# A two-layer encoder with grouped experts: the overflow branch placed at the layer's end

## The chip, the core and the metric

The kernel runs on one core of a Trainium2 chip. The core has five engines that run their own instruction queues side by side and wait for each other by semaphores: TensorE (PE, matrix products), VectorE (DVE), ScalarE (ACT), GpSimd (POOL) and SyncE (SP), which here only issues transfers. Transfers run on 16 DMA engines. The metric is the device time of one execution in microseconds; the median of several runs counts.

## The reference

The program is two layers over 512 tokens of width 1024, all in float32. A layer has a mixer and a grouped mixture of experts, each with a residual sum and a layer norm:

```
for i in range(DEPTH):                      # DEPTH = 2
    z = x @ w_in                            # token mixer and query of a memory attention
    o = concat([tok, xa]) @ w_out[i]
    x = layer_norm(ALPHA * x + o)
    f = grouped_moe(x, router_w, router_b, w_gate[i], w_up[i], w_down[i])
    x = layer_norm(ALPHA * x + f)

def grouped_moe(x, ...):                    # 16 experts in 4 groups, two experts per token
    ...                                     # sigmoid scores, best group, top 2 inside it
    for e in range(N_EXPERTS):
        h = jax.nn.silu(xt @ w_gate[e]) * (xt @ w_up[e])
        out = out + combine[:, e:e + 1] * (h @ w_down[e])
```

`w_gate` and `w_up` are 1024 x 512 per expert and layer, `w_down` 512 x 1024: 6 MB of weights per expert, 16 experts, two layers.

## The kernel before

**Experts.** Each expert takes up to 128 tokens. `route` and `tables` make for every expert a list of its tokens' rows (`idxs`) and their gates. `experts` (L650) then runs the 16 experts in a loop: `gather(e)` fetches the tokens' rows from DRAM through GpSimd, `xtrans(e)` transposes them on TensorE and splits them, `gate_up(e)` makes gate and up and multiplies them into `h`, `htrans(e)` transposes `h` into `ht`, `down(e)` makes the down product, and `scatter(e)` adds its rows to a copy of the residual stream in DRAM, `rd[i]`. `down(e - 1)` comes behind `gate_up(e)`; in the last expert it comes in the middle of `gate_up(15)`. The last expert's own product isn't scattered: `selt`, a matrix of ones and zeros that says which token sits in which of its slots, is made from `posp`, and `total` (L781) adds on TensorE the rows read back from `rd[i]`, and `selt` times the product.

**Precision.** Every product is made of three (`mm3`, L202 to L204): both operands are split into a high part that TensorE's fast float32 mode takes and a low rest. ScalarE makes the high part (a copy, L168 for weights, L207 for activations), VectorE the rest (a subtraction, L169 and L208).

**Weights.** A `Stream` W loads weights in tiles of 1 MB (`raw`) through SyncE, in the order of use, into pages of on-chip memory; there are 24 pages for everything. `W.keep` is the number of pages that loads must leave free, `W.flight` the number of loads under way, `W.stop` how many tiles of the next layer wait until its end. `W.rings(8)` sets pages aside for split tiles (`high`, `low`). Whenever a tile's use ends, `W.done` calls `pump`, which splits the next raw tile and issues the next load.

**More than 128 tokens.** `overflow` counts on TensorE (L603) how many tokens each expert has and makes `nover`, the number of full sets of 128 over the first, on VectorE (L605 to L610). `more` (L893 on) loads `nover` into a register of every engine's queue, compares it with zero, and only if it is larger runs a loop that handles the rest, one expert at a time, with gathers, products, weight loads of its own and a scatter-add to `rd[i]`. In the profiled execution no instruction of that loop's body ran: each queue jumps over it. Before, `more` is called between `fill` and the expert loop, with the page `hy` for its scratch. `fill` is in layer 0 the keys and values of the next layer's memory attention (`keys_values`, L315), in layer 1 nothing.

**The order of the work.** A planner of the compiler orders each engine's instructions by a simulated timeline, earlier program text first where it can. `tc.issue_after(ins)` keeps what a block issues behind `ins` on that instruction's engine. Inside `tc.manual_schedule(...)` the listed engines keep the program's order. The expert loop is in such a block for TensorE, ScalarE and VectorE; before, `order.close()` ends it ahead of the last expert, whose gate, up and `down(14)` the planner orders freely. The layer's end (from `htrans(last)` on) is in a second such block, with eight small warm-up products (`keep_warm(8)`) held behind the last product of gate and up. A conditional block is one unit for the planner: nothing from outside is put among its instructions.

Of the kernel before, what the change touches and what calls it, by code (L numbers as in the profile page):

```python
# [18 lines left out]
FT = mybir.dt.float32  # L19
FR = mybir.dt.float32r  # L20
# [3 lines left out]
OP = mybir.AluOpType  # L24
# [3 lines left out]
P = 128  # L28
D = 1024
KB = D // P  # L30
S = 512
NC = S // P
# [5 lines left out]
FE = 512  # L38
# [9 lines left out]
def trunk(ctx, tc, x, mem, w_in_a, sgu_ln_g, sgu_ln_b, sgu_w, sgu_b, w_in_b, conv_w, w_kv, w_out,  # L48
          ln1_g, ln1_b, router_w, router_b, w_gate, w_up, w_down, ln2_g, ln2_b, out):
    nc = tc.nc  # L50
    vec, act, pool_e, pe, sp = nc.vector, nc.scalar, nc.gpsimd, nc.tensor, nc.sync
# [12 lines left out]
    def page(name, shape, dtype=FT, of=None):  # L64
        of = free_pages if of is None else of
        assert of, f"no page for {name}; held: {sorted(v[1] for v in held.values())}"
        i = of.pop(0)
        uid[0] += 1
        t = pages.tile(shape, dtype, name=f"{name}_{uid[0]}", tag=f"pg{i}", bufs=1)
        held[id(t)] = (i, name, t)  # L70
        return t

    def drop(*ts):
        for t in ts:
            i, name, _ = held.pop(id(t))
            W.home(name).append(i)
# [4 lines left out]
    def bank(shape, name="bank"):  # L81
        return psum.tile(shape, FT, name=name, tag="B", bufs=3)
# [115 lines left out]
    W = Stream()  # L198

    def mm3(o, a, b, start, stop):  # L200

        pe.matmul(o, a[0], b[0], start=start, stop=False)  # L202
        pe.matmul(o, a[0], b[1], start=False, stop=False)  # L203
        return pe.matmul(o, a[1], b[0], start=False, stop=stop)  # L204
# [7 lines left out]
    ident = consts.tile([P, P], FT, name="ident")  # L212
# [40 lines left out]
    slot1 = consts.tile([P, P], FT, name="slot1")  # L253
# [41 lines left out]
    def keep_warm(n):  # L295

        t = bank([P, 4, P], "warm")
        for _ in range(n):
            pe.matmul(t, ones_b, ones_b[:, None, :].to_broadcast([P, 4, P]), start=True, stop=True)
# [12 lines left out]
    memh = page("memh", [P, KB, NMEM], FR)  # L312
    meml = page("meml", [P, KB, NMEM], FR)
# [5 lines left out]
    def keys_values(after=None):  # L319
        kt = page("kt", [P, 2, H, NMEM], FR)  # L320
        vt = page("vt", [P, 2, 2, MW], FR)
        a = [acc("ka") for _ in range(H)]
        for j in range(4):
            g = W.next()
            for kk in range(2):
                k = 2 * j + kk
                for h in range(H):
                    cs = slice(h * P, (h + 1) * P)
                    mm3(a[h][:, :NMEM], (g[:, 0, kk, cs], g[:, 1, kk, cs]), (memh[:, k, :], meml[:, k, :]),
                        k == 0, k == KB - 1)  # L330
            W.done(g)
        for h in range(H):
            split_to(kt[:, 0, h, :], kt[:, 1, h, :], a[h][:, :NMEM])
        a = [acc("va") for _ in range(2)]
        for j in range(4):
            g = W.next()
            for kk in range(2):
                k = 2 * j + kk
                for m in range(2):
                    ms = slice(m * P, (m + 1) * P)  # L340
                    with ExitStack() if after is None or j < 3 else tc.issue_after(after):
                        mm3(a[m], (memh[:, k, ms], meml[:, k, ms]), (g[:, 0, kk, :], g[:, 1, kk, :]),
                            k == 0, k == KB - 1)
            W.done(g)
        for m in range(2):
            split_to(vt[:, 0, m, :], vt[:, 1, m, :], a[m])
        return kt, vt

    def x_transposed():
        xh = [page("xh", [P, 4, S], FR) for _ in range(2)]  # L350
# [155 lines left out]
    posp = consts.tile([P, NC, E], FT, name="posp")  # L506
# [144 lines left out]
    def experts(i, lnp, fill, after, stop, fine=False):  # L651

        last = E - 1
        xg = page("xg", [P, 2, D])
        pool_e.memset(xg, 0.0)
        hy = page("h", [P, 4, FE])
# [15 lines left out]
        def xtrans(e):  # L672
            for q in range(2):
                t = bank([P, 4, P], "xt")
                for k in range(4):
                    k0 = 4 * P * q + 2 * P * (k // 2) + k % 2
                    pe.transpose(t[:, k, :], xg[:, e % 2, k0:k0 + 2 * P - 1:2], ident)  # L677
                split_to(xt[:, 0, 4 * q:4 * q + 4, :], xt[:, 1, 4 * q:4 * q + 4, :], t)
# [26 lines left out]
        def down(e, evict):  # L705
            for n in range(2):
                o = acc("ya")
                for j in range(2):
# [5 lines left out]
                        evict(n, o)  # L714
                    W.done(g)

        def scaled(e):
            return lambda n, o: act.activation(ys[e % 2][:, n * 512:(n + 1) * 512], o, AF.Copy, scale=tabs[e][1])  # L718

# [2 lines left out]
        if i:  # L722
            with tc.issue_after(last_entry[-1]):
                keep_warm(8)
        fill()
        more(i, hy)
        W.keep, W.flight = 0, 4
        W.ahead, W.whole, W.on_pool = 6, True, lambda n: False
        W.rings(8)
        xtrans(0)  # L730
        gather(2)
        W.pump()
        order = ExitStack()
        order.enter_context(tc.manual_schedule(engines={ET.PE, ET.Activation, ET.DVE}))
        for e in range(E):
            if e == last:
                order.close()
            up = gate_up(e, (lambda: (down(last - 1, scaled(last - 1)), scatter(last - 1))) if e == last else None)
            if e + 1 < E:
                xtrans(e + 1)  # L740
            if e + 3 < E:
                gather(e + 3)
            if e == 5:
                W.parts += 2
            if 0 < e < last:
                down(e - 1, scaled(e - 1))
                scatter(e - 1)
            if e == last - 3:
                W.keep = 4
                W.stop = stop - 2 if stop else 0  # L750
            if e == last:
                W.rings(0)
                drop(xt, xg)
                selp = page("selt", [P, 2, NC, P], FT)
                for c in range(NC):
                    vec.tensor_scalar(selp[:, 0, c, :], slot1, posp[:, c, last:last + 1], None, op0=OP.is_equal)
                t = bank([P, NC, P], "selt")
                for c in range(NC):
                    pe.transpose(t[:, c, :], selp[:, 0, c, :], ident)
                selt = page("selr", [P, NC, P], FR)  # L760
                vec.tensor_copy(selt, t)
                drop(selp)
                xs[:] = [page("x", [P, 2, D]) for _ in range(2)]
                xrow[:] = [xs[c // 2][:, c % 2, :] for c in range(NC)]
                with tc.issue_after(added[last - 1].ins):
                    lnp = ln_params(*lnp, pool_e)
                for c in range(NC):
                    W.behind = sp.dma_start(xrow[c], rd[i][c * P:(c + 1) * P, :]).ins
            if e < last:
                htrans(e)  # L770
# [63 lines left out]
            moments(c)  # L834

        with tc.manual_schedule(engines={ET.PE, ET.Activation, ET.DVE, ET.Pool}):
            with tc.issue_after(up.ins):
                keep_warm(8)
            htrans(last)
            keep_warm(4)  # L840
            down(last, parts)
            act.activation(lnp[:, 0], lnp[:, 0], AF.Copy, scale=ALPHA)
            if fine:
                for c in range(3):
                    total(c)
                half_moments(0)
                part(1, 0)
                finish(0, "pool")
                after(0)
                part(1, 1)  # L850
                total(3)
                moments(1)
                centred(1)
                finish(1, "both")
                after(1)
                half_moments(2)
                centred(2)
                finish(2, "split")
                after(2)
                half_moments(3)  # L860
                centred(3)
                finish(3, "vec")
                after(3)
            else:
                total(0)
                total(1)
                half_moments(0)
                centred(0)
                finish(0, "dve")
                total(2)  # L870
                half_moments(1)
                centred(1)
                finish(1, "dve")
                after(0)
                total(3)
                W.after = after(1).ins
                half_moments(2)
                if "both" != "pool":
                    centred(2)
                finish(2, "both")  # L880
                half_moments(3)
                if "split" != "pool":
                    centred(3)
                finish(3, "split")
# [95 lines left out]
    W.after = last_mem.ins  # L980
    W.pump()
    W.after = None
    kt, vt = keys_values()
    xh, xl = x_transposed()
    for c in range(NC):
        transposed(xrow[c], KB, lambda q: xh[q], lambda q: xl[q], c * P)
# [5 lines left out]
    t = bank([P, 12], "cwt")  # L992
    pe.transpose(t, cwr, ident[:12, :12])
    act.activation(cw.rearrange("p t b -> p (t b)"), t, AF.Copy)
    t = bank([P, H, P], "sgt")
# [78 lines left out]
    def fill0():  # L1074
        W.on_pool = lambda n: False
        kv1.append(keys_values(last_entry[-1]))
        drop(memh, meml)
    xhl = []

    def next_x(c):  # L1080
# [2 lines left out]
        xh, xl = xhl[0]  # L1083
        return transposed(xrow[c], KB, lambda q: xh[q], lambda q: xl[q], c * P)
    experts(0, (ln2_g[0], ln2_b[0]), fill0, next_x, stop)
    kt, vt = kv1[0]
    xh, xl = xhl[0]


# [69 lines left out]
```

## Time and profile before

| | |
|---|---|
| three timed runs | 1032.32, 1035.75, 1035.86 us; median 1035.75 |
| profiled execution | 1031.97 us, of which the span from first to last instruction is 1030.1 us |
| TensorE busy | 983.7 us (95%), weight loads of TensorE 810.6 us (79%) |
| VectorE, ScalarE, GpSimd busy | 774.2 (75%), 627.7 (61%), 200.5 us (19%) |
| mean granted clock of TensorE | 0.973 |
| moved by DMA | 273.30 MB, mean 265 GB/s |
| expert loop, layer 0 and layer 1 | about 213 to 500 us and 706 to 998 us of the span |

Times in rows are microseconds from the span's start. A timeline row has start, duration, engine, line, operation, what it writes and reads, how many instructions were merged, and in brackets the idle time ahead of it with what ended it. PE is TensorE, PEld its weight loads, a q behind an engine's name its queue's own instructions (register loads, branches, semaphores, DMA issues). Durations of matrix products overlap: one of 0.39 us starts 0.23 us after the one before it.

### The profile page before, as it was taken

Reading aid. Unit: us, or ns where it says so; the run is one execution under the profiler, and the core shown is the slowest. Engines: PE = TensorE matmul, PEld = TensorE weight load, DVE = VectorE, ACT = ScalarE, POOL = GpSimd, SP = SyncE. Lnnn points to the kernel's source line nnn. Section 1 sums busy time; section 2 is a strip of 40 time slices with the busy share of each in tenths; the row PEclk is TensorE's granted clock in tenths of the full one; section 3 lists DMA queues with packets and bytes.
Section 4 is the critical chain, followed back from the end, with each engine's and each line's share of the span. In section 5 each row is a group of like instructions: output and inputs, shape, how many; then the busy total and the mean of one; then the engine's idle time right before and its main releaser. Section 6 shows DMA issues by size and latency. Waiting matters only on the chain. (4 is left out here: it accounts for less than half of the span.)

```text
span 1030.1 us, 12721 instructions
## 1 busy us (share of the span) xinstructions
PE 983.7 (95%) x4815; PEld 810.6 (79%) x4816; DVE 774.2 (75%) x884; ACT 627.7 (61%) x684; POOL 200.5 (19%) x111
## 2 busy tenths in 40 slices
PE   8999999969999999999999999977899999999995
PEld 6788888858888888888679887865688888888873
DVE  4738567867989898898894455675689898988975
ACT  4626532556788787878643414233687887878763
POOL 0000002112332413321110000221133324233023
PEclk9999999989999999999999999987899999999998
DMA  9813266667999999999880425490799999999944
GB/s 321 294 42 123 91 237 247 244 225 265 364 367 333 366 360 360 360 357 362 282 320 1 164 82 207 131 396 25 232 330 362 372 327 383 359 362 355 357 87 160
DMA packets 102219, 273.30 MB, mean 265 GB/s; under 512 B 10442, under 2 KB 10966, under 8 KB 102152
## 3 DMA queue, kind: packets, MB, share of 16 engines
q1 hardware_dynamic: 89480, 242.84, 64.5%
q0 software_dynamic: 11808, 26.97, 9.4%
q10 hardware_dynamic: 864, 2.62, 0.7%
q8 instruction: 39, 0.64, 0.2%
q14 instruction: 28, 0.23, 0.1%
HBM read 262.22 MB, written 26.21 MB: 280 GB/s over the span
## 5 line engine op out<-in xcount | busy, mean ns | idle before, releaser
L169 DVE TENSOR_TENSOR low<-raw,high 128x2048 fp32r<-128x2048 f32 x189 | 427.9, 2288 | 80.9 <-ACT high L168 79.4
L168 ACT ACTIVATE high<-raw 128x2048 fp32r<-128x2048 f32 x189 | 355.1, 1910 | 22.7 <-PE ga L204 10.1
L668 POOL DMA_INDIRECT xg<-x1d,idxs x32 | 83.2, 2601 | 299.6 <-PE xt L677 270.5
L168 ACT ACTIVATE split<-raw 128x1024 fp32r<-128x1024 f32 x66 | 68.9, 1058 | 71.1 <-PE za L204 26.0
L202 PE MATMUL ya<-high,ht 128*128 128x512 f32 x256 | 103.8, 406 | 0.0
L169 DVE TENSOR_TENSOR split<-raw,split 128x1024 fp32r<-128x1024 f32 x61 | 73.6, 1221 | 39.6 <-ACT split L168 38.9
L204 PE MATMUL ga<-high,xgt 128*128 128x512 f32 x248 | 99.1, 399 | 2.9 <-DVE xgt L208 2.9
L204 PE MATMUL ya<-high,ht 128*128 128x512 f32 x256 | 101.3, 396 | 0.1
L203 PE MATMUL ya<-low,ht 128*128 128x512 f32 x256 | 101.1, 395 | 0.0
L202 PE MATMUL ga<-high,xgt 128*128 128x512 f32 x248 | 100.7, 406 | 0.1
L203 PE MATMUL ga<-low,xgt 128*128 128x512 f32 x248 | 98.4, 397 | 0.0
L204 PE MATMUL ua<-high,xgt 128*128 128x512 f32 x248 | 97.1, 392 | 0.0
L202 PE MATMUL ua<-high,xgt 128*128 128x512 f32 x248 | 96.9, 391 | 0.0
L203 PE MATMUL ua<-low,xgt 128*128 128x512 f32 x248 | 96.8, 390 | 0.0
L169 POOL TENSOR_TENSOR split<-raw,split 128x1024 fp32r<-128x1024 f32 x5 | 11.9, 2383 | 267.0 <-DVE sto L475 147.0
L202 PE MATMUL za<-xh,split 128*128 128x512 f32 x160 | 61.6, 391 | 2.0 <-ACT xh L207 2.0
L203 PE MATMUL za<-xl,split 128*128 128x512 f32 x160 | 62.5, 391 | 0.0
L204 PE MATMUL za<-xh,split 128*128 128x512 f32 x160 | 61.5, 389 | 0.0
L204 PEld LDWEIGHTS ga<-high,xgt 128*128 128x128 f32 x248 | 47.4, 191 | 14.1 <-DVE xgt L208 4.0
L204 PEld LDWEIGHTS ya<-high,ht 128*128 128x128 f32 x256 | 48.1, 188 | 12.8 <-DVE ht L208 1.3
L664 POOL DMA_INDIRECT rd<-h,idxs x16 | 40.4, 2523 | 89.3 <-ACT h L718 79.6
L202 PEld LDWEIGHTS ya<-high,ht 128*128 128x128 f32 x256 | 48.4, 189 | 10.5 <-ACT ht L207 0.6
(250 smaller groups left out, 1886.2 us busy)
## 6 DMA issues: line engine op xcount, KB each, us to landing
raw<-in_w_gate_dram SPq DMA_DIRECT2D x64, 1024.0 KB, 9.8
raw<-in_w_up_dram SPq DMA_DIRECT2D x64, 1024.0 KB, 9.6
raw<-in_w_down_dram SPq DMA_DIRECT2D x64, 1024.0 KB, 10.5
raw<-in_w_kv_dram SPq DMA_DIRECT2D x8, 1024.0 KB, 7.4
raw<-in_w_out_dram SPq DMA_DIRECT2D x8, 1024.0 KB, 8.0
raw<-in_w_in_b_dram SPq DMA_DIRECT2D x8, 1024.0 KB, 11.1
raw<-in_w_in_a_dram SPq DMA_DIRECT2D x6, 1024.0 KB, 5.4
x1d<-x POOLq DMA_DIRECT2D x8, 512.0 KB, 6.0
```

The source lines that it names most:

```text
L168: act.activation(high, src, AF.Copy)
L169: (pool_e if self.on_pool(self.count) else vec).tensor_tensor(low, src, high, op=OP.subtract)
L202: pe.matmul(o, a[0], b[0], start=start, stop=False)
L203: pe.matmul(o, a[0], b[1], start=False, stop=False)
L204: return pe.matmul(o, a[1], b[0], start=False, stop=stop)
L664: added[e] = pool_e.indirect_dma_start(out=rd[i], out_offset=bass.IndirectOffsetOnAxis(ap=tabs[e][0], axis=0), in_=ys[e % 2], in_offset=No ...
L668: pool_e.indirect_dma_start(out=xg[:, e % 2], out_offset=None, in_=x1d[i], in_offset=bass.IndirectOffsetOnAxis(ap=tabs[e][0], axis=0), bou ...
```

## The change

The call of `more` moves from ahead of the expert loop to the layer's end, behind the last expert's gate and up and ahead of the loads of the rows from `rd[i]`, and gets a page of its own. With the branch gone from the start, layer 0's first transposes are held behind the last product of `keys_values` by `issue_after`. The block in the program's order now closes behind the last expert's gate, up and `down(14)`. The last expert's slots are compared on VectorE at the start of expert 14 and transposed at the start of expert 15, and one page more is kept free from expert 12 on.

```diff
@@ keys_values @@
-                        mm3(a[m], (memh[:, k, ms], meml[:, k, ms]), (g[:, 0, kk, :], g[:, 1, kk, :]),
-                            k == 0, k == KB - 1)
+                        end = mm3(a[m], (memh[:, k, ms], meml[:, k, ms]), (g[:, 0, kk, :], g[:, 1, kk, :]),
+                                  k == 0, k == KB - 1)
...
-        return kt, vt
+        return kt, vt, end.ins
@@ experts @@
+        def last_slots():
+
+            selp = page("selt", [P, 2, NC, P], FT)
+            for c in range(NC):
+                vec.tensor_scalar(selp[:, 0, c, :], slot1, posp[:, c, last:last + 1], None, op0=OP.is_equal)
+            return selp
+
+        def last_tokens(selp):
+
+            t = bank([P, NC, P], "selt")
+            for c in range(NC):
+                pe.transpose(t[:, c, :], selp[:, 0, c, :], ident)
+            selt = page("selr", [P, NC, P], FR)
+            vec.tensor_copy(selt, t)
+            drop(selp)
+            return selt
...
-        fill()
-        more(i, hy)
+        end = fill()
...
-        xtrans(0)
+        with ExitStack() if i else tc.issue_after(end):
+            xtrans(0)
...
         for e in range(E):
+            if e == last - 1:
+                selp = last_slots()
             if e == last:
-                order.close()
+                selt = last_tokens(selp)
             up = gate_up(e, (lambda: (down(last - 1, scaled(last - 1)), scatter(last - 1))) if e == last else None)
...
             if e == last - 3:
-                W.keep = 4
+                W.keep = 5
...
             if e == last:
                 W.rings(0)
                 drop(xt, xg)
-                selp = page("selt", [P, 2, NC, P], FT)
...
-                drop(selp)
+                order.close()
+                rest = page("more", [P, 4, FE])
+                more(i, rest)
+                drop(rest)
                 xs[:] = [page("x", [P, 2, D]) for _ in range(2)]
...
         with tc.manual_schedule(engines={ET.PE, ET.Activation, ET.DVE, ET.Pool}):
-            with tc.issue_after(up.ins):
-                keep_warm(8)
+            keep_warm(8)
             htrans(last)
```

The callers only hand the third value of `keys_values` through (`fill0` returns it, the others drop it).

## Rows read from the trace of the kernel before

**Rows 1.** Stretch: PE, PEld, DVE, ACT, POOL busy (instructions), clock, DMA share, GB/s
```profile
200.00:216.00 16.00, 7.59 (x39) 6.11 (x38) 9.80 (x18) 8.12 (x8) 2.44 (x3) 0.84 0.59 198
780.00:940.00 160.00, 160.00 (x752) 132.78 (x751) 140.76 (x91) 129.34 (x108) 49.73 (x19) 1.00 1.00 361
```

**Rows 2.** Timeline around layer 0's branch: start, duration, engine, line, operation, idle before
```profile
204.17 1.08 POOL L668 DMA_INDIRECT xg<-x1d,idxs  x1 [22.48 <-DVE gates L635]
...
205.80 4.50 DVE L169 TENSOR_TENSOR low<-raw,high 128x2048 fp32r<-128x2048 f32 x2 [2.38 <-ACT high L168]
...
211.73 0.14 DVE L610 CAST nover<-ovn 1x1 int32<-1x1 f32 x1
212.94 1.28 ACT L207 ACT_TABLE_LOAD   x1 [6.38 <-ACTq L894]
...
213.43 1.95 PE L677 MATMUL xt<-ident,xg 128*128 128x128 f32 x8 [7.40 <-DVEq L894]
...
215.20 0.69 DVE L208 TENSOR_TENSOR xgt<-xt,xgt 128x512 fp32r<-128x512 f32 x1 [3.33 <-ACT xgt L207]
...
216.24 0.63 PE L204 MATMUL ga<-split,xgt 128*128 128x512 f32 x1
...
217.86 0.39 PE L202 MATMUL ga<-split,xgt 128*128 128x512 f32 x1
```

**Rows 3.** First gather, from issue to landing: layer 0, then layer 1
```profile
DMA to landing us min/median/max: 4.2/4.2/4.2
...
DMA to landing us min/median/max: 4.3/4.3/4.3
```

**Rows 4.** Timeline around layer 1's branch, and the stall at its second expert
```profile
701.36 1.08 POOL L668 DMA_INDIRECT xg<-x1d,idxs  x1 [6.09 <-DVE gates L635]
...
706.02 1.95 PE L677 MATMUL xt<-ident,xg 128*128 128x128 f32 x8 [2.12 <-PEq L894]
...
710.22 2.29 DVE L169 TENSOR_TENSOR low<-raw,high 128x2048 fp32r<-128x2048 f32 x1 [0.88 <-PE ga L204]
...
724.21 1.11 PE L702 MATMUL htr<-ident,h 128*128 128x128 f32 x4 [3.51 <-DVE h L693]
```

**Rows 5.** The branch's instructions on TensorE's queue in layer 1
```profile
L893 PEldq TENSOR_LOAD <-nover x1: 312/312/312, 704.6 to 704.6; - x1
...
L894 PEldq COMPARE_BRANCH  x1: 318/318/318, 705.1 to 705.1; - x1
```

**Rows 6.** Waits of SyncE's queue: us in total, times, longest
```profile
SPq L894 <- SPq L894: 7.5, 3, 6.4
```

**Rows 7.** Timeline at layer 1's end, from the last product of "up" to the sums
```profile
998.04 1.90 PE L299 MATMUL warm<-ones_b 128*128 128x512 bf16 x8
998.31 0.69 DVE L693 TENSOR_TENSOR h<-h,ua 128x512 f32<-128x512 f32 x1 [0.69 <-PE ua L204]
998.91 2.28 DVE L169 TENSOR_TENSOR low<-raw,high 128x2048 fp32r<-128x2048 f32 x1
...
999.78 0.60 PE L702 MATMUL htr<-ident,h 128*128 128x128 f32 x4
...
1000.99 2.13 SPq L768 DMA_DIRECT2D x<-rd  x3
...
1007.10 1.02 PE L785 MATMUL ra<-x,ident 128*128 128x512 f32 x2
```

**Rows 8.** Timeline of VectorE at layer 0's end
```profile
501.31 2.28 DVE L169 TENSOR_TENSOR low<-raw,high 128x2048 fp32r<-128x2048 f32 x1
...
503.51 0.68 DVE L208 TENSOR_TENSOR ht<-htr,ht 128x512 fp32r<-128x512 f32 x1
...
505.24 2.29 DVE L169 TENSOR_TENSOR low<-raw,high 128x2048 fp32r<-128x2048 f32 x1 [1.05 <-ACT high L168]
```

**Rows 9.** Waits of SyncE's queue in layer 0's loop: 222 to 420, then 440 to 460
```profile
SPq L147 <- DVE low L169: 119.9, 47, 7.9
...
SPq L147 <- DMA raw<-in_w_up_dram: 11.1, 3, 4.7
```

More of the change, by code (lines that the diff above doesn't have):

```diff
@@ L753, in experts @@
                 drop(xt, xg)
-                selp = page("selt", [P, 2, NC, P], FT)
[L755 to L761, printed above, removed]
-                drop(selp)
+                order.close()
+                rest = page("more", [P, 4, FE])
+                more(i, rest)
+                drop(rest)
                 xs[:] = [page("x", [P, 2, D]) for _ in range(2)]
@@ L982, in trunk @@
     W.after = None
-    kt, vt = keys_values()
+    kt, vt, _ = keys_values()
     xh, xl = x_transposed()
@@ L1077, in fill0 @@
         drop(memh, meml)
+        return kv1[0][2]
     xhl = []
@@ L1085, in trunk @@
     experts(0, (ln2_g[0], ln2_b[0]), fill0, next_x, stop)
-    kt, vt = kv1[0]
+    kt, vt, _ = kv1[0]
     xh, xl = xhl[0]
```

## The prediction, made before the changed kernel was run

> **What bounds the kernel now.** I read the page's first two parts, then the stretches of each stage, then the instructions around the branch and at both layers' ends, and last the waits of the load queue. In the page TensorE is busy 95% of 1030.1 us; by stretches it works without a gap through nearly all of both expert loops (160.00 of 160.00 us between 780 and 940, granted clock 1.00, VectorE 140.76) [rows 1]. What this change can win or lose is therefore TensorE's idle time at the loops' two ends, unless it slows the loop itself.
>
> At the start of layer 0's loop the branch holds everything. The memory projection ends near 206.0; TensorE's next work is the first transposes at 213.43, 7.40 us idle, released by VectorE's queue at the branch. The branch needs `nover`, and VectorE makes it last, at 211.87, behind two subtractions of split weights (4.50 us from 205.80) [rows 2]. In that stretch TensorE works 7.59 of 16 us and the clock averages 0.84 [rows 1]. The first gather is issued at 204.17 and lands 4.2 us later, so at 208.4 its rows were there, 5.0 us before anyone was allowed to use them [rows 2, 3].
>
> Layer 1 looks alike and is not. The load of `nover` into TensorE's register starts at 704.6 [rows 5] and the transposes at 706.02, but the gather is issued at 701.36 and lands 4.3 us later, at 705.66 [rows 3, 4]. The branch costs 0.36 us there. The 3.51 us that TensorE waits later, before 724.21, begin with a subtraction at 710.22 that waits for TensorE's first gate tile (for its page), so this chain moves only when TensorE's start moves [rows 4].
>
> **The change, part by part.**
>
> *Layer 0's start.* The load of the register, the compare, the jump and the small steps that make `nover` leave TensorE's path. What is late next? TensorE may transpose at 208.4. Its third matrix product, however, needs the low half of the transposed tokens, a subtraction on VectorE (0.69 us) that started at 215.20; the product followed at 216.24 [rows 2]. VectorE's two weight subtractions wait for pages that the projection frees near 205.8, before the tokens are there, so I expect the planner to leave them and the two value subtractions in front: VectorE is then free at 211.9, where it made `nover`, the low half is done at 211.9 + 0.69 = 212.6, and the third product moves from 216.24 to 212.6: -3.6 us. If the tokens go between the two weight subtractions, VectorE is free for them about 2.3 us earlier (half of 4.50), and the gain is 5.9. On the other side stands the clock: after the 7.4 us of idle the product at 216.24 takes 0.63 us and the one at 217.86 0.39, the lower and the higher level [rows 2]. TensorE would still be idle for some 2.4 us and then again until 212.6, and the clock may fall all the same and stay low for longer than it does now; eight more products at 0.24 us extra take 1.9 from the gain. Bounds -1.7 and -5.9; I take -3.6, nearest to the order that the trace has.
>
> *Layer 1's start.* The gather's landing is the next wait: -0.3 us, between 0 and -0.4. ScalarE's table load behind the branch (1.28 us in layer 0 [rows 2]) goes too, beside other work.
>
> *The loop.* It starts earlier as a whole. Loads in layer 0 wait first for pages that VectorE frees (119.9 us of waits from 222 to 420), later for earlier loads alone (from 440 on) [rows 9]: DMA becomes the tighter stream, and its slack shrinks. Since its first loads in the loop wait for VectorE, they move with TensorE, and the later state is the same one, shifted. I cost the loop at nothing; if that cover fails, the gain at layer 0's start comes back as stalls at its end, up to +3.6. One page more kept back for the last three experts: those loads wait for earlier loads, not pages, so nothing. The slots' comparisons and transposes move from expert 15 to 14: same instructions, and VectorE has 19 us in 160 free [rows 1].
>
> *Layer 1's end.* The branch now stands between the last product of "up" and the last expert's down product. Its price on TensorE's queue: load 0.31, compare and jump 0.32, and from 704.6, where the load starts, to the next instruction at 706.02 it is 1.4 us in all [rows 4, 5]. Before, eight warm-up products began at 998.04, the moment the last product was through, and transposes followed at 999.78 [rows 7]. After, the warm-up is in program order behind the branch: 998.04 + 1.4, and everything behind it, down product, sums, normalization, stores, is 1.4 later; no gap stands before the sums at 1007.10 that could take it up. VectorE also loses the planner's order: the last weight subtraction (2.28 us) comes before the product `h`, not after (998.31 against 998.91 [rows 7]). It starts where VectorE idles for 0.69 us ahead of 998.31 [rows 7], so `h` ends at 997.62 + 2.28 + 0.69 = 1000.6 instead of 999.0, still before 1001.2, when TensorE would take it. Queued behind the branch on SyncE are the loads of the rows; these wait for the last scatter-add anyway and start at 1000.99 [rows 7]. Cost +1.4; at least 0 (if TensorE meets the branch while it waits for something else), at most 2.5.
>
> *Layer 0's end.* The same 1.4 on TensorE, but VectorE has more in front of the branch. Program order there is: weight subtraction, `h`, one more subtraction for the next layer's first weights, branch, low half of `ht`. In the trace the planner put that subtraction behind `ht` (505.24 behind 503.51) [rows 8]. `h` and the weight subtraction of 501.31 only change places; what stands newly in front of `ht` is that other subtraction, 2.29, and the branch, 1.0 (ScalarE's took 1.07, from `nover` to its table load at 212.94 [rows 2]), together 3.3, less 0.3 because the first subtraction doesn't wait for "up" as `h` does: +3.0 us, and the down product's third step waits for it. If the planner sets the branch elsewhere, 0.5; at most 4.
>
> Sum: -3.6 - 0.3 + 3.0 + 1.4 = +0.5 us. The profiled execution took 1031.97 (span 1030.1 and 1.9 around it), so 1032.5 by that account. The three timed runs lie at 1032.32, 1035.75 and 1035.86; with the profiled one, two near 1032 and two near 1035.8. I cannot tell which way the next median falls, take the middle, 1034.0, and predict 1034.5.
>
> **Rivals.**
>
> *A missed jump on the path (slower).* SyncE's queue waited three times for itself at the old branch, 7.5 us in all and 6.4 the longest, while TensorE's needed 1.4 for everything [rows 4, 6]; SyncE had no free page then, and nobody missed it. At the layer's end ScalarE, VectorE and TensorE are all on the path, and one of them pausing as SyncE did costs 6.4 less the 1.0 to 1.4 already counted: +5 to 1039.5 for one, 1044.5 for both layers. For it: that row. Against: SyncE's part of the body, with 24 loads, is the longest to jump over. It decides as soon as a pause on one of these three exceeds about 5 us. The Trainium skill ("Runtime: NRT & Kernel Launch", Instruction fetch mechanics) has a rule that speaks for this rival: a taken branch whose target isn't in the pages of code already fetched stalls until the page has come. SyncE's row agrees with it; by it alone each of the three engines could pay this at each layer's end.
>
> *The start gains more and the ends are hidden (faster).* Token subtractions between the weight ones (-5.9), -0.3, and each branch met while the engine waits for `h` or the rows, +0.4 each: -5.4, 1028.6. For it: greedy planning and idle time before 205.80. Against: the planner's own order in [rows 2].
>
> *The branch isn't where the text puts it.* It is one unit for the planner, which may set later work ahead of it, as the trace shows for weight splits in front of the old branch [rows 2]. Then layer 0's order on VectorE stays mild, the ends cost 0.5 + 0.5, sum -2.9: 1031.1.
>
> **How the numbers follow.** Forecast 0.50, branch elsewhere 0.10, faster rival 0.22, slower rival 0.18. A measurement of this kernel tells about 0.5% (5.2 us) from no change. The faster rival lies on that border: three quarters of it and a little of the others make 0.21 faster; most of the slower one and a tail of the forecast's make 0.20 slower; 0.59 between. For the likeliest alone the start's bounds put the sum between -1.8 and +2.4, and the runs scatter by 1.8 to either side of 1034.0: 1030.4 to 1038.2. Up to the edges of both rivals it is 1028.5 to 1040.
>
> **What will show it.** TensorE's gap before layer 0's first transposes: 2.4 instead of 7.4 us. VectorE's token subtraction there: near 211.9 (right) or before 210 (faster rival). Behind the last "up" product: 1.4 us without work on TensorE in both layers. Layer 0's `ht` subtraction about 3 us further behind "up" than before. A queue's self-wait over 5 us on ScalarE, VectorE or TensorE speaks for the slower rival. The forecast is wrong if TensorE has gaps in the middle of a loop, or if layer 1's start moves by more than half a us.

## The result and the profile after

The changed kernel took 1037.05 us (median of 16 runs, 1034.75 to 1039.24), the kernel before 1032.34 in the same runs (16 runs, 1029.28 to 1035.86): a ratio of 1.0052, 95% interval 1.0038 to 1.0065. It is slower by 0.5%, 4.7 us; 1034.5 had been predicted, half a microsecond over a base of 1034.0, so no difference that can be told. The base was 1.7 us above the 1032.34 that the kernel before took beside it: by luck that brings the absolute figure nearer (2.6 us off) than the difference (4.2 off). The profiled execution has a span of 1035.4 us, 5.3 more than before.

The loops are what they were. Columns as in [rows 1], which the first and third line answer:

```profile
200.00:216.00 16.00, 11.14 (x47) 8.43 (x47) 10.19 (x19) 8.37 (x8) 3.50 (x3) 0.80 0.63 219
500.00:524.00 24.00, 22.47 (x79) 13.71 (x79) 13.76 (x24) 9.24 (x14) 0.00 (x0) 0.86 1.03 377
780.00:940.00 160.00, 160.00 (x753) 132.75 (x752) 140.94 (x91) 128.35 (x108) 49.03 (x18) 1.00 1.01 361
```

TensorE works more at layer 0's start (11.14 us in place of 7.59) and has no gap in the middle of a loop; new is a granted clock of 0.86 where layer 0 ends.

Layer 0's start, which answers to [rows 2] (timeline: start, duration, engine, line, operation, idle before):

```profile
205.69 4.50 DVE L169 TENSOR_TENSOR low<-raw,high 128x2048 fp32r<-128x2048 f32 x2 [2.40 <-ACT high L168]
...
208.18 1.20 PE L677 MATMUL xt<-ident,xg 128*128 128x128 f32 x8 [2.25 <-DMA xg<-x1d,idxs]
...
211.42 1.27 DVE L208 TENSOR_TENSOR xgt<-xt,xgt 128x512 fp32r<-128x512 f32 x2
...
212.14 0.80 PE L204 MATMUL ga<-split,xgt 128*128 128x512 f32 x1 [1.39 <-DVE xgt L208]
```

TensorE's gap is 2.25 us and ends with the gather, and the third product comes at 212.14 in place of 216.24.

Layer 0's end, which answers to [rows 8], with TensorE's rows added:

```profile
493.44 4.50 DVE L169 TENSOR_TENSOR low<-raw,high 128x2048 fp32r<-128x2048 f32 x2 [0.51 <-ACT high L168]
...
495.93 0.39 PE L204 MATMUL ua<-high,xgt 128*128 128x512 f32 x1
497.85 0.68 DVE L693 TENSOR_TENSOR h<-h,ua 128x512 f32<-128x512 f32 x1
498.45 2.28 DVE L169 TENSOR_TENSOR low<-raw,high 128x2048 fp32r<-128x2048 f32 x1
...
500.84 3.60 PE L299 MATMUL warm<-ones_b 128*128 128x512 bf16 x8 [4.53 <-DVEq L907]
...
504.23 1.06 PE L702 MATMUL htr<-ident,h 128*128 128x128 f32 x4
...
505.96 0.69 DVE L208 TENSOR_TENSOR ht<-htr,ht 128x512 fp32r<-128x512 f32 x1 [5.23 <-ACT ht L207]
```

And the branch's instructions there (count, ns, first and last start), TensorE's queue and then VectorE's; they answer to [rows 5]:

```profile
L907 PEldq EVENT_SEMAPHORE  x2: 51/51/51, 496.4 to 496.6; - x2
...
L907 PEldq COMPARE_BRANCH  x1: 228/228/228, 493.6 to 493.6; - x1
```
```profile
L907 DVEq EVENT_SEMAPHORE  x2: 21/21/21, 500.8 to 500.9; - x2
```

TensorE's last "up" product ends at 496.3. Its jump is through at 496.6, because its queue had read and compared `nover` while the products still ran. But the warm-up behind the jump starts at 500.84, when VectorE jumps, and VectorE jumps only after two weight subtractions, `h`, and a third subtraction. After 4.53 us without work the eight warm-up products take 3.60 us, where those of [rows 7] take 1.90: the clock is at its lower level. Then come the transposes, then `ht`.

Layer 1's end, answering to [rows 7]: the same wait, 2.33 us, and the clock is still up behind it (1.90 us for eight products):

```profile
998.14 4.49 DVE L169 TENSOR_TENSOR low<-raw,high 128x2048 fp32r<-128x2048 f32 x2 [0.51 <-ACT high L168]
1002.55 0.68 DVE L693 TENSOR_TENSOR h<-h,ua 128x512 f32<-128x512 f32 x1
...
1003.35 1.90 PE L299 MATMUL warm<-ones_b 128*128 128x512 bf16 x8 [2.33 <-DVEq L907]
...
1005.08 0.60 PE L702 MATMUL htr<-ident,h 128*128 128x128 f32 x4
```

Where the 5.3 us went is read by setting TensorE's instructions of two traces side by side. The table gives, in us against the profile before, what each stage adds: A up to the transposes of `h` in expert 14 of layer 0; B to those of expert 15; C to the first token transposes of layer 1; D to expert 14 of layer 1; E to expert 15; F to the first sum (each number is the difference of two starts, after minus before, less that of the stage ahead). The profiled executions of the four kernels marked * are 1.8 to 2.1 us late from 42 us on, at instructions that are the same in all; their granted clock is 0.83 between 40 and 50 us, where the others but one have 1.00. That is scatter of single executions, and it stands in A. The one, that of the warm-up in other buffers, is 3.2 us late from 64 us on for a reason of its own, told with it, and regains 1.9 at layer 0's start. In the kernels marked w the eight warm-up products left their place behind the last "up" product (both ends; in "only layer 0's branch moved" that of layer 1 alone): the first experiment shows what that does to B, E and F.

| kernel | A | B | C | D | E | F | median us | ratio to before (95%) |
|---|---|---|---|---|---|---|---|---|
| changed | -4.3 | +6.4 | +2.3 | -1.1 | +2.0 | -0.1 | 1037.1 | 1.0052 (1.0038 to 1.0065) |
| no branch * w | -2.5 | +2.5 | +2.2 | -0.9 | +2.0 | +1.3 | 1034.6 | 1.0028 (1.0011 to 1.0044) |
| warm-up in other buffers | -2.9 | +3.0 | +1.4 | -0.9 | +0.4 | 0.0 | 1035.1 | 1.0032 (1.0019 to 1.0045) |
| subtractions behind | -6.4 | +1.5 | +1.0 | -1.5 | +1.2 | -0.1 | 1029.7 | 0.9981 (0.9969 to 0.9994) |
| only layer 0's branch moved w | -4.6 | +6.3 | +2.4 | -1.1 | +2.0 | +1.3 | 1038.2 | 1.0057 (1.0037 to 1.0077) |
| order alone * w | -0.3 | +2.4 | +4.6 | +0.4 | +2.0 | +1.2 | 1041.4 | 1.0092 (1.0067 to 1.0116) |
| move alone * | -2.3 | +7.9 | +1.8 | +0.3 | +2.2 | 0.0 | 1039.7 | 1.0070 (1.0047 to 1.0092) |
| behind, branch at the start * w | +2.9 | +1.0 | +1.1 | -0.7 | +0.6 | +0.2 | 1034.5 | 1.0027 (1.0011 to 1.0044) |
| behind, warm-up ahead | -4.9 | +0.6 | +1.1 | -1.1 | +0.1 | 0.0 | 1028.1 | 0.9963 (0.9945 to 0.9981) |
| the same, layer 0's branch alone | -4.6 | +0.6 | +1.0 | -0.8 | -0.4 | -0.1 | 1027.6 | 0.9963 (0.9947 to 0.9979) |
| the same, 4 pages kept | -4.3 | +0.6 | -0.1 | -0.1 | -0.5 | -0.1 | 1027.6 | 0.9965 (0.9950 to 0.9980) |

### The profile page after: what moved, and what is told of

It is laid out like the page before. It is cut to its first block, busy times and chain, and to the rows that moved or that the text cites. A ratio compares the mean times of both kernels' runs of the same rounds, so it can differ in the third digit from the quotient of the medians.

```text
span 1035.4 us, 12714 instructions
## 1 busy us (share of the span) xinstructions
PE 984.5 (95%) x4815; PEld 811.0 (78%) x4816; DVE 773.4 (75%) x884; ACT 625.3 (60%) x682; POOL 200.2 (19%) x111
## 5 line engine op out<-in xcount | busy, mean ns | idle before, releaser
L204 PEld LDWEIGHTS ya<-high,ht 128*128 128x128 f32 x256 | 48.1, 188 | 12.1 <-DVE ht L208 0.4
L207 ACT ACTIVATE xgt<-xt 128x512 fp32r<-128x512 f32 x64 | 34.8, 595 | 37.1 <-PE xt L677 37.1
```

What stands on the lines that cost most here:

```text
L207: r = act.activation(hi, src, AF.Copy)
```

## The experiments

The first four ran together, the next four, and the last two; the kernel before ran beside each lot (medians 1032.2, 1030.8, 1031.7), so the ratios compare better than the times. Three accounts of the loss compete: "join" (TensorE waits behind the branch for VectorE's jump), "own price" (TensorE's own load, compare and jump) and "order" (VectorE's program order in the last expert).

**No branch.** The two calls of the branch are left out, and so is the handling of tokens beyond an expert's slots, which this data doesn't enter.

```diff
                 rest = page("more", [P, 4, FE])
-                more(i, rest)
                 drop(rest)
```

> The changed kernel with the overflow branch left out at both layers (its body is never entered with this data); the last expert's program order stays. Theory 'join': in the changed kernel TensorE's warm-up behind the branch takes a PSUM buffer whose last reader, by the program, is VectorE inside the body that is never entered; it therefore waits until VectorE itself has jumped (500.84 us in layer 0, 1003.3 in layer 1), long after TensorE's own jump (496.6 and 1001.2). Without the branch the warm-up starts within 0.3 us of the last 'up' product in both layers, the transposes of h follow h (498.6 and 1003.2 instead of 504.2 and 1005.1), the clock does not fall in layer 0: -7.5 to -8.5 us, 1028.5 to 1029.5. Rival 'own price': the loss is TensorE's own load, compare and jump, 1.4 us per layer: -2.8, 1034.2. Rival 'order': VectorE's program order alone delays h and ht, branch or not: at most -1, 1036.

1034.57 us, 2.5 below the changed kernel: that is the size of "own price", but not its mechanism. The timeline of TensorE in layer 0, then in layer 1:

```profile
484.14 1.90 PE L299 MATMUL warm<-ones_b 128*128 128x512 bf16 x8
...
502.11 0.66 PE L702 MATMUL htr<-ident,h 128*128 128x128 f32 x4 [2.28 <-DVE h L693]
...
985.12 1.90 PE L299 MATMUL warm<-ones_b 128*128 128x512 bf16 x8
...
1003.09 0.83 PE L702 MATMUL htr<-ident,h 128*128 128x128 f32 x4 [2.28 <-DVE h L693]
```

No instruction waits for a jump now, but more than the branch went. The change had dropped the `issue_after(up.ins)` around `keep_warm(8)`; in the changed kernel the branch holds the warm-up behind "up". Without it the planner put the eight products into the middle of the last expert, where they are through some 14 us before the last "up" product. There they delay what follows: from expert 14's transposes to `h` it is 20.85 us (19.10 in the changed kernel). Then TensorE waits 2.28 us for `h`, which stands on VectorE behind two subtractions, with nothing to fill the wait, and in layer 1 what follows runs at the lower clock (four warm-up products in 1.91 us, in place of 1.03: F +1.3). Behind "up" the warm-up would lie in that wait, which would give back these 1.75 us in each layer and perhaps the 1.3: about 1030, close to "join". That is an estimate; no run leaves the branch out alone, so this one doesn't speak against "join".

**The warm-up in other buffers.** One edit aims at the wait that "join" names; `keep_warm` is called in other places too, and their targets move with it.

```diff
-        t = bank([P, 4, P], "warm")
+        t = acc("warm").rearrange("p (k s) -> p k s", s=P)
```

> The changed kernel; only the warm-up's target moves to the other group of PSUM buffers, which in the body are read last by ScalarE, not by VectorE. Theory 'join': the warm-up now waits for ScalarE's jump (497.6 in layer 0, 1000.5 in layer 1) and starts at 497.7 and 1001.3 instead of 500.84 and 1003.35; the transposes still need VectorE's jump and start at 501.0 and 1003.5 instead of 504.2 and 1005.1: -3.2 and -1.7, about 1032.2, and VectorE's jump is now what the transposes wait for. Rival 'own price': no wait on VectorE matters, 0: 1037. Rival 'order': the transposes wait for h anyway, at most -1: 1036.

The trace does what "join" says. TensorE's rows at layer 0's end:

```profile
498.92 1.89 PE L299 MATMUL warm<-ones_b 128*128 128x512 bf16 x8 [1.28 <-ACTq L907]
502.27 0.63 PE L702 MATMUL htr<-ident,h 128*128 128x128 f32 x4 [1.46 <-DVEq L907]
```

The warm-up waits for ScalarE's jump, the transposes for VectorE's, and the clock stays up: B falls from 6.4 to 3.0, E from 2.0 to 0.4. In time it brings 2.0 us by the medians (1035.06), not the 4.9 expected. Most of the difference may lie at the kernel's start, where the edit also moved warm-up products: the ten and the eight that stood apart before run as one block, TensorE then waits 1.63 us for a split weight, and from 64 us on everything is 3.2 us late.

```profile
1.30 6.26 PE L299 MATMUL warm<-ones_b 128*128 128x512 bf16 x18 [1.30 <-DVE ones_b L252]
...
11.71 0.38 PE L202 MATMUL ka<-memh,split 128*128 128x256 f32 x1 [1.63 <-ACT split L168]
```

The profiled execution was the fastest of the twelve (1032.74), so that share is read from one profile and not shown for the median.

**The subtractions behind `ht`.** From the middle of the last expert on no weight is split until the transposes of `h` are issued; one full tile (in layer 0 more) so comes behind `h` and the jump, in half tiles.

```diff
+                        if half and e == last:
+                            W.hold = True
...
             keep_warm(8)
-            htrans(last)
+            W.after = htrans(last).ins
+            W.hold = False
+            W.pump()
+            W.after = None
```

> The changed kernel; the last weight subtractions of the last expert (one of its second down tile, and in layer 0 the one for the next layer) are made behind ht instead of in front of h and the branch. Theory 'join': VectorE then reaches its jump right behind h, which follows the last 'up' product; TensorE's warm-up starts about 1.4 us behind that product (497.7 instead of 500.84 in layer 0, about 1002 instead of 1003.35 in layer 1), the clock stays up: -4.6 and -1.5, about 1031. Rival 'own price': TensorE's jump costs the same: 0, 1037. Rival 'order': VectorE's h and ht come earlier here too, so it says the same as 'join' (-4 to -6).

1029.68 us: 7.4 below the changed kernel, more than expected, and 0.19% below the kernel before (0.06 to 0.31). Layer 0's end:

```profile
494.28 0.69 DVE L695 TENSOR_TENSOR h<-h,ua 128x512 f32<-128x512 f32 x1 [0.69 <-PEq L912]
...
498.50 0.69 DVE L208 TENSOR_TENSOR ht<-htr,ht 128x512 fp32r<-128x512 f32 x1 [3.53 <-ACT ht L207]
```
```profile
495.50 1.90 PE L299 MATMUL warm<-ones_b 128*128 128x512 bf16 x8 [1.32 <-DVEq L912]
```

`h` now waits for TensorE, not TensorE for `h`; the branch still holds the warm-up in its place, and 1.32 us remain between "up" and the warm-up. "Own price" is out. Some 2 us of stage A are luck of this profile: the clock came up 1.8 us sooner at the loop's start.

**Only layer 0's branch moved.** Layer 1's stands ahead of its loop again.

```diff
         end = fill()
+        if i:
+            more(i, hy)
...
-                more(i, rest)
+                if not i:
+                    more(i, rest)
```

> The changed kernel with layer 1's branch put back to its old place ahead of the loop; layer 0's stays at the layer's end. Theory 'join': layer 1's end gives back its 2.0 to 2.3 us, layer 1's start takes 0.3: -1.9, 1035.1. Rival 'own price': -1.4 + 0.3 = -1.1, 1036. If layer 1's start takes 2 us or more (the loop's first products wait for VectorE at the old place), no gain: 1037.

1038.22 us: no gain (stage E the same +2.0), against both theories as they stood; layer 1's start didn't take it (0.2 us). Without a jump at layer 1's end TensorE waits there for `h` (2.28 us), as in the kernel without a branch, and the warm-up has left its place as there (it starts at 986.93, the last "up" product ends at 1002.6). By the same estimate (1.75 and 1.3 us) it would be about 1035.2 with the warm-up in place, what "join" had said, so the run decides nothing between the two. It made VectorE's order the suspect, which the next two take apart.

**Order alone and move alone.** In the first both branches go back ahead of the loops and all else of the change stays; in the second the planner gets the last expert back and the branch stays at the end.

```diff
         end = fill()
+        more(i, hy)
...
-                more(i, rest)
```
```diff
             if e == last:
+                order.close()
                 selt = last_tokens(selp)
...
-                order.close()
                 rest = page("more", [P, 4, FE])
```

> The changed kernel with both branches back at their old places ahead of the loops; all else of the change stays (last expert in program order, slots in expert 14, one page more kept). Theory 'order': the loss at the layers' ends is made by VectorE's program order, which puts two weight subtractions (4.5 us) in front of h; the run without any branch shows TensorE idle 2.28 us for h in both layers with the clock falling after it, +2.1 in layer 0 and +3.4 in layer 1 against the kernel before; the start is that of before: about 1037.7. Theory 'join' (TensorE waiting for VectorE's jump is the loss): no jump stands there, so the time of before, 1032 to 1033. Rival 'own price': as 'join'.

> The changed kernel with the last expert's gate, up and the down product between them given back to the planner; the branch stays at the layer's end. The planner now puts h ahead of the subtractions, but in layer 0 two of them (4.5 us) still stand between h and the jump; in layer 1 one stands in front of h and none behind it before the jump. Theory 'join': layer 0 loses as much as in the changed kernel (the warm-up waits for VectorE's jump near 501), layer 1 gains 1.5 to 2: about 1035.2. Theory 'order' alone (only what stands in front of h counts): layer 0 gains 5 as well, about 1030.5. Rival 'own price' (TensorE's jump): 1037.

The order alone costs 0.92% (0.67 to 1.16), 9.5 us, more than the whole change. TensorE waits 2.28 us for `h` at both ends, and C and F grow beside it. But here too nothing holds the warm-up (486.31 and 990.91), and the same estimate gives it 3.5 us of B and E and the 1.2 of F: about 4.8 of the 9.5 are left for the order, and C's +4.6 has no explanation. "Join" alone, which allowed nothing, is out by that rest. The move alone fails too, 1039.7 us: `h` stands well, but two subtractions behind it keep VectorE from its jump. VectorE, then TensorE, at layer 0's end:

```profile
499.17 0.69 DVE L693 TENSOR_TENSOR h<-h,ua 128x512 f32<-128x512 f32 x1 [0.69 <-PEq L907]
499.77 4.49 DVE L169 TENSOR_TENSOR low<-raw,high 128x2048 fp32r<-128x2048 f32 x2
```
```profile
504.37 3.60 PE L299 MATMUL warm<-ones_b 128*128 128x512 bf16 x8 [5.31 <-DVEq L907]
```

So "order" alone is out too, which had said 1030.5. Both hold at once: what TensorE needs of VectorE is `h` where no jump stands, and the jump where one does; a weight subtraction in front of that leaves TensorE idle as far as the warm-up doesn't fill the time.

**Warm-up ahead of the branch, and layer 0's branch alone.** On top of the subtractions behind `ht`; the warm-up now stands inside the block in the program's order, which keeps it behind "up" with a branch or without:

```diff
             if e == last:
                 W.rings(0)
                 drop(xt, xg)
+                keep_warm(8)
                 order.close()
...
-            keep_warm(8)
             W.after = htrans(last).ins
```

> The kernel with the last subtractions behind ht (run before: 1029.7), and the warm-up in front of the branch instead of behind it. Theories 'join' and 'order' both: the warm-up now lies beside VectorE's h and jump, so the transposes follow the later of the two jumps, 1.0 to 1.5 us earlier per layer, if the idle time between warm-up and transposes does not lower the clock: 1027 to 1028.5; if it does, no gain: 1029.7. 'Own price': the warm-up no longer hides anything, 0.

> As the one before, with layer 1's branch back ahead of its loop (layer 1's end then has the new order and no jump). 'Join': layer 1's end gains up to 1.4 more, its start loses 0.3: 1026 to 1028. 'Order': what counts was already gone, 0 to -0.5 against the one before.

1028.14 and 1027.64 us, ratios of 0.9963 both; the intervals overlap that of the run before (0.9981), so the step of some 2 us isn't clear of noise. The row that matters is TensorE's:

```profile
497.90 0.63 PE L704 MATMUL htr<-ident,h 128*128 128x128 f32 x4 [0.45 <-PEq L912]
```

The transposes wait 0.45 us for TensorE's own jump, and for nobody else. Where VectorE arrives in time it is all one whether layer 1's branch stands at the start or at the end.

**The fourth cell.** The subtractions behind, both branches at their old places (the edit of the order alone and that of the subtractions together).

> The last subtractions behind ht, as in the run at 1029.7, but both branches at their old places ahead of the loops: the fourth cell of branch place by order. If the two parts of the change add up, the branch's move is worth the same -4.3 here as between the changed kernel and the one with the order alone (1037.1 against 1041.4): about 2.1 us slower than before, 1033 to 1034.5. If the loss at the ends was all in front of h and the jump, and the branch's move pays its 4.3 only in part (its own jump at the end costs 1.4 per layer), the difference to the run at 1029.7 is 1.5 to 3: 1031 to 1032.5. If the move is worth nothing once the order is right: 1029.7.

1034.47 us. By ratios, in per cent of the kernel before:

| | branch at the start | branch at the end |
|---|---|---|
| subtractions in front of `h` | +0.92 | +0.52 |
| subtractions behind `ht` | +0.27 | -0.19 |

By rows the move is worth 0.40 and 0.46 points (4.1 and 4.7 us), by columns the order 0.65 and 0.71 (6.7 and 7.3 us). They look as if they added up, as the first expectation had it, but the table doesn't show it. The intervals of the four ratios are 0.13 to 0.25 points to either side, and in both kernels of the left column the warm-up has left its place. Its price can be read at layer 1's end, where this kernel and the one at 1027.64 differ only in that; this one first:

```profile
988.10 1.90 PE L299 MATMUL warm<-ones_b 128*128 128x512 bf16 x8
...
1004.65 0.66 PE L704 MATMUL htr<-ident,h 128*128 128x128 f32 x4 [0.85 <-DVE h L695]
```
```profile
993.82 1.90 PE L299 MATMUL warm<-ones_b 128*128 128x512 bf16 x8
995.56 0.60 PE L704 MATMUL htr<-ident,h 128*128 128x128 f32 x4
```

From expert 14's transposes (984.49 and 976.42) that is 20.16 against 19.14 us: 1.0 per layer. So about 2.0 of the 4.7 us are the warm-up's and 2.7 the branch's (an estimate), which is the second expectation's 1.5 to 3. In the upper row the share estimated above for the order alone (3.5 and 1.2 us) would leave nothing of the 4.1: by these estimates the move pays only where VectorE reaches its jump early. No run has the branch at the start, the new order, and the warm-up in its place.

**Four pages kept.** `W.keep = 5` set back to 4 in the fastest version.

> The kernel with the warm-up ahead, the subtractions behind ht and layer 0's branch alone at the end (1027.6), with 4 pages kept back for the last experts as before the change, instead of 5. TensorE lost 1.1 us between 536 and 540 us of the changed kernel's layer 1, at transposes that wait for VectorE; if the page kept back holds up the next layer's weights and so shifts VectorE's work there: -1, 1026.6. If it is VectorE's order of the normalization: 0, 1027.6.

1027.57 us, no difference. In the profile TensorE's stall at 534 us shrinks (one wait of 0.59 us in place of two of 0.84 and 0.69), C falls by 1.1 and D gives 0.7 of it back: the first token transposes of layer 1 take 1.95 us in this profile, 1.20 in the other. Four pages or five are equal here.

## Why the prediction was wrong

*Layer 0's start, -3.6: right.* VectorE's token subtraction stood at 211.42 (forecast 211.9), the third product at 212.14 (212.6), the gap of 7.40 us became 2.25. The clock stayed low until 216.2, so the first expert was only 2.7 us early; from the second on it was 4.5. In the medians this can't be seen alone: the pairs of the table above have the warm-up in them.

*Layer 1's start, -0.3: the right wait, but no gain.* The next wait is the gather's landing (TensorE idle 2.15 us for it at 710.42); with the old place the same transposes come within 0.2 us. From the products that count for `nover` to these transposes it is 2.42 us before and 2.41 after.

*The loop, 0: right.* 4.5 us ahead at the second expert, 4.3 at the fifteenth.

*Layer 0's end, +3.0: the step that failed; it measured +6.4 to the transposes and +6.9 to the sums.* The prediction let two things run side by side: "the same 1.4 on TensorE", and on VectorE one more subtraction and the branch in front of `ht`. The 1.4 was read off a place where TensorE had to wait for `nover` and its own work [rows 5]; at the layer's end its queue runs ahead, and the jump ends 0.3 us behind its last product (0.45 in the row above). VectorE's side, forecast at +3.0, was cheaper: it is through its jump at 500.9, in the time of before 505.2 (4.3 later), and `ht` stood at 503.51 there [rows 8]; that alone would be +1.7. But the two are in series. TensorE's first instruction behind the branch needs VectorE's jump, by a dependence that exists only on the path never taken (the PSUM buffer of the warm-up is one that the body reads on VectorE); behind it come the warm-up, slowed by the idle time it waited out, the transposes and `ht`, which VectorE awaits for 5.23 us with nothing to do. The prediction named this wait at the old branch [rows 2] as VectorE being late with `nover`, and did not ask who would be late at the new one.

*"`h` and the weight subtraction of 501.31 only change places": not free either.* It was costed at nothing. Where no jump stands (order alone) the transposes come 2.4 us later with that exchange; 1.75 of it is the displaced warm-up by the estimate above, and 0.7 is left.

*Layer 1's end, +1.4: measured +2.0, for another reason.* It was put on TensorE's jump, which covers `h` until 1001.2 in the forecast. That cover isn't there; what was late is VectorE.

*Between the layers: not in the prediction.* Of C's +2.3, 0.6 lies ahead of the first sum, where the first products behind the warm-up run at the lower clock; 1.1 went away with the fourth page in the fastest kernel; the rest stays open. D gives 1.1 back.

The slower rival named the wrong mechanism. SyncE's queue again waited for itself, 7.1 us at the longest, and nobody for it:

```profile
SPq L907 <- SPq L907: 10.2, 3, 7.1
```

At the layers' ends the longest such wait was 0.45 us on TensorE and 1.20 on VectorE (move alone), none of the 5 that the rival needed. The stall of a taken branch that the Trainium skill describes ("Runtime: NRT & Kernel Launch", Instruction fetch mechanics) does not show on the engines that matter here.

## What to carry to other kernels

A branch that is never taken is still a meeting point: what reuses a buffer of the skipped body waits for the jump of the engine that would have used it there (4.53 us for VectorE, with other buffers 1.28 for ScalarE). So ask of each engine what stands in its queue ahead of that jump, not what the jump costs. Work that nobody waits for yet (the next weights' subtractions) belongs behind the meeting point or behind the product that feeds the next stage; program order put it in front here. A sum of two engines' delays has to say whether they lie side by side or in a chain: here that was 3.0 against 6.9 us. And whoever takes a block out should look at what it held in place: without the branch the warm-up ran some 14 us too early, and four of the comparisons above measure that along with what they were meant for.

## What had not been expected of the hardware

- TensorE's load, compare and jump, 1.4 us at the old place, cost 0.3 to 0.45 us behind a long run of products: the queue compares while the products run (compare at 493.6, last product's end at 496.3).
- The clock: after 4.53 or 5.31 us without work the eight warm-up products took 3.60 us; after 2.33, 1.78, 1.52 and 1.32 us, 1.90 us, and the four products behind the transposes then 1.03. Where 2.28 us of idle time stood ahead of the transposes and no warm-up between, these four took 1.91, 1.91, 1.83, 1.27 and once 1.03 us (five such places).
- In four of the twelve profiles the first 45 us take 1.8 to 2.1 us more than in seven of the others, with the same instructions. One profile can't carry a difference of that size; stages of it, taken as differences between instructions, can.
